# Rolling the columns of an 8192 x 8192 matrix: the heads of the rows spread over the copy

## The chip, the cores and the metric

One core of one Trainium2 chip runs the kernel. The metric is the device time of one execution in microseconds; the time before is the median of three runs.

## The reference

The input is a float32 matrix of 8192 x 8192 (268 MB), rolled by 100 columns to the right:

```python
def setup_inputs():
    return {"x": np.random.randn(8192, 8192).astype(np.float32), "shift": 100}

def reference(x, shift):
    return np.roll(x, shift, axis=1)
```

So `out[r, 100:8192] = x[r, 0:8092]` and `out[r, 0:100] = x[r, 8092:8192]`. Nothing is calculated; 268.44 MB are read and 268.44 MB are written.

## The kernel before

With `s = 100`, the kernel sets `a = 256`: of each output row, the columns from 256 on are the "long piece" (7936 columns, 31.7 KB), and the first 256 columns, 1 KB, are the "head". `g = a - s = 156` is how many columns of the head come from the start of the same input row; the other 100 come from the end of it.

**The copy of long pieces (L36 to L43).** It goes from DRAM to DRAM directly. Rows are taken in `blocks = 128` blocks of 64 rows. A block is four transfers (`j`), each of 16 rows, with SP issuing the even ones and ACT the odd ones (`engines[j % 2]`). So each queue issues two 496 KB transfers to a block. In the last four blocks each transfer is cut in two at column `mid`. There are 528 transfers in all, and each of the two engines issues its own in order.

**The heads (L60 to L80).** POOL issues all their transfers, and they go through SBUF. A stage `k` is 512 rows: 128 partitions of `Q = 4` neighbouring rows, and there are `n_st = 16` stages. The end of row r and the start of row r + 1 lie side by side in memory, so one read can take both.

- L72 reads into tile `t` three pieces of 1 KB for each partition: the last 100 columns of a row together with the first 156 of the next (384 KB).
- L73 reads the last 100 columns of the partition's fourth row into tile `h` (50 KB), and L76 the first 156 columns of its first row (78 KB).
- L74 and L77, two copies on DVE, put the two parts of each piece of `t` into their places in `h`. `h` is then four heads of 1 KB for each partition.
- L80 stores `h` into the first 256 columns of 512 output rows (512 KB).

The stages' reads are all issued first, in one loop (L67 to L78), and the stores after them in a second loop (L79, L80). Each pool has 16 buffers, one for each stage, so that no stage waits for the buffers of another. POOL runs its instructions in the order of the program. In the program all copies of long pieces stand ahead of all heads; since they are on other engines, the heads start at once, beside the copy.

Of the kernel before, what the change touches and what calls it, by code (L numbers as in the profile page):

```python
# [1 line left out]

# [4 lines left out]


@with_exitstack
def kernel(  # L10
    ctx: ExitStack,
    tc: tile.TileContext,
    x: bass.AP,
    shift: int,
    out: bass.AP,
):
    nc = tc.nc
    n_rows, n_cols = x.shape
    s = shift % n_cols
    a = -(-s // 128) * 128  # L20
    if 0 < a <= 384 and a + 128 <= n_cols:
        a += 128
    g = a - s
    P = nc.NUM_PARTITIONS
    engines = [nc.sync, nc.scalar]
    n_chunks = 16
    rows = n_rows // n_chunks

    xm = x.rearrange("(c e j) w -> c j e w", e=16, j=4)
    om = out.rearrange("(c e j) w -> c j e w", e=16, j=4)
    if a < n_cols:  # L36
        blocks = n_rows // 64
        mid = (a + n_cols) // 256 * 128
        for c in range(blocks):
            parts = ((a, mid), (mid, n_cols)) if c >= blocks - 4 and a < mid else ((a, n_cols),)  # L40
            for j in range(4):
                for lo, hi in parts:
                    engines[j % 2].dma_start(out=om[c, j, :, lo:hi], in_=xm[c, j, :, lo - s:hi - s])  # L43
    if a == 0:
        return


    if a > 512:
        for i in range(n_chunks):
            r = slice(i * rows, (i + 1) * rows)  # L50
            nc.gpsimd.dma_start(out=out[r, :s], in_=x[r, n_cols - s:])
            if g > 0:
                nc.gpsimd.dma_start(out=out[r, s:a], in_=x[r, :g])
        return

    Q = 4  # L60
    n_st = n_rows // (P * Q)
    reads = ctx.enter_context(tc.tile_pool(name="reads", bufs=n_st))
    heads = ctx.enter_context(tc.tile_pool(name="heads", bufs=n_st))
    xt = x.rearrange("(k p q) c -> k p q c", q=Q, p=P)
    ot = out.rearrange("(k p q) c -> k p q c", q=Q, p=P)
    tiles = []
    for k in range(n_st):  # L67
        t = reads.tile([P, Q - 1, a], x.dtype)
        h = heads.tile([P, Q, a], x.dtype)
        lead = bass.AP(tensor=x.tensor, offset=(k * P * Q + 1) * n_cols - s,  # L70
                       ap=[[Q * n_cols, P], [n_cols, Q - 1], [1, a]])
        nc.gpsimd.dma_start(out=t[:], in_=lead)  # L72
        nc.gpsimd.dma_start(out=h[:, Q - 1, :s], in_=xt[k, :, Q - 1, n_cols - s:])  # L73
        nc.vector.tensor_copy(h[:, :Q - 1, :s], t[:, :, :s])  # L74
        if g > 0:
            nc.gpsimd.dma_start(out=h[:, 0, s:], in_=xt[k, :, 0, :g])  # L76
            nc.vector.tensor_copy(h[:, 1:, s:], t[:, :, s:])  # L77
        tiles.append(h)  # L78
    for k, h in enumerate(tiles):  # L79
        nc.gpsimd.dma_start(out=ot[k, :, :, :a], in_=h[:])  # L80


# [1 line left out]
_INS = ['x', 'shift']  # L84
_OUTS = [((8192, 8192), 'float32')]

_NUMBERS = {'shift': 100}


# [26 lines left out]
```

## Time and profile before

| | |
|---|---|
| time, median of 3 runs | 816.8 us (815.75 to 818.27) |
| span of the profiled execution | 828.0 us |
| instructions in the profile | 689 |
| DMA packets | 22278, 276.90 MB, mean 334 GB/s |
| first and last read of heads issued (L72) | 1.3 and 240.4 us |
| first and last store of heads issued (L80) | 242.2 and 379.6 us |
| long piece of 496 KB, issue to landing, median | 12.7 us |
| read into `t`, issue to landing, median | 50.6 us |
| store of `h`, issue to landing, median | 108.2 us |
| POOL busy | 41.3 us; an L72 762 ns, L73 559 ns, L76 542 ns, L80 724 ns on average |
| DVE busy | 12.3 us; L74 382 ns, L77 467 ns on average |

The profiled execution is one of its own; its span is 1.4% over the median of the runs. Times within it are counted from the span's start. A DMA queue's row gives packets, megabytes and the time its packets took as a share of what 16 DMA engines have in the span: q1 and q10 carry the long pieces of SP and ACT, and q0 carries what POOL issues. GB/s in the profile counts each byte moved once, so a byte that goes from DRAM to DRAM counts once though it is read and written there. A row of waits names the waiting instruction, what it waited for, the microseconds in total, how many times, and the longest.

### The profile page before, as it was taken

How to read it: one execution, taken by the hardware profiler on the slowest of the kernel's cores; microseconds unless marked ns; L12 is line 12 of the kernel's file. 1: busy time of each engine (PE TensorE's matmuls, PEld its weight loads, DVE VectorE, ACT ScalarE, POOL GpSimd, SP SyncE). 2: the span in 40 equal slices, each digit the busy share in tenths (PEclk: the TensorE clock that was granted, in tenths of full speed). 3: DMA queues.
4: the chain of work that ended last, by engine and by line, in shares of the span. 5: the costliest groups of instructions: out<-in, count | busy, mean ns of one | idle time of the engine just before them, and what ended most of it. 6: DMA issues, size and time to landing. Idle time of an engine off the chain costs nothing. (4 is left out here: it accounts for less than half of the span.)

```text
span 828.0 us, 689 instructions
## 1 busy us (share of the span) xinstructions
DVE 12.3 (1%) x32; POOL 41.3 (5%) x68
## 2 busy tenths in 40 slices
DVE  0000000000010000000000000000000000000000
POOL 2011000000021100000000000000000000000000
DMA  9999999999999999999999999999999999999998
GB/s 308 340 350 334 344 340 337 337 339 344 337 342 348 352 351 345 354 339 346 347 341 344 333 325 325 319 330 333 330 324 322 335 330 328 322 331 328 327 314 300
DMA packets 22278, 276.90 MB, mean 334 GB/s; under 512 B 9473, under 2 KB 9729, under 8 KB 13825
## 3 DMA queue, kind: packets, MB, share of 16 engines
q1 hardware_dynamic: 8448, 130.04, 46.1%
q10 hardware_dynamic: 8448, 130.04, 44.7%
q0 software_dynamic: 5376, 16.78, 8.4%
q14 instruction: 6, 0.04, 0.0%
HBM read 268.44 MB, written 268.44 MB: 648 GB/s over the span
## 5 line engine op out<-in xcount | busy, mean ns | idle before, releaser
L80 POOL DMA_DIRECT2D out_dram<-h x16 | 11.5, 724 | 126.6 <-DMA out_dram<-h 86.8
L76 POOL DMA_DIRECT2D h<-in_x_dram x16 | 8.7, 542 | 141.4 <-DMA t<-in_x_dram 141.4
L72 POOL DMA_DIRECT2D t<-in_x_dram x16 | 12.2, 762 | 30.8 <-DMA h<-in_x_dram 30.0
L73 POOL DMA_DIRECT2D h<-in_x_dram x16 | 8.9, 559 | 39.9 <-DMA h<-in_x_dram 39.9
L74 DVE COPY h<-t 128x300 f32<-128x300 f32 x16 | 6.1, 382 | 260.2 <-DMA t<-in_x_dram 260.2
L77 DVE COPY h<-t 128x468 f32<-128x468 f32 x16 | 7.5, 467 | 0.0
L97 POOL MEMSET const-float32-0.0<- 128x1 f32 x1 | 0.1, 99 | 0.2 <-issue 0.2
L97 POOL MEMSET const-bfloat16-1.0<- 128x1 bf16 x1 | 0.1, 102 | 0.0
L97 POOL MEMSET const-float32-1.0<- 128x1 f32 x1 | 0.1, 99 | 0.0
L97 POOL MEMSET const-uint8-127<- 128x1 uint8 x1 | 0.1, 99 | 0.0
## 6 DMA issues: line engine op xcount, KB each, us to landing
out_dram<-in_x_dram ACTq DMA_DIRECT2D x248, 496.0 KB, 12.7
out_dram<-in_x_dram SPq DMA_DIRECT2D x248, 496.0 KB, 12.7
out_dram<-h POOLq DMA_DIRECT2D x16, 512.0 KB, 108.2
t<-in_x_dram POOLq DMA_DIRECT2D x16, 384.0 KB, 50.6
out_dram<-in_x_dram SPq DMA_DIRECT2D x16, 248.0 KB, 6.0
out_dram<-in_x_dram ACTq DMA_DIRECT2D x16, 248.0 KB, 5.9
h<-in_x_dram POOLq DMA_DIRECT2D x16, 78.0 KB, 43.2
h<-in_x_dram POOLq DMA_DIRECT2D x16, 50.0 KB, 49.9
```

The lines of the kernel that those rows point to most:

```text
L72: nc.gpsimd.dma_start(out=t[:], in_=lead)
L73: nc.gpsimd.dma_start(out=h[:, Q - 1, :s], in_=xt[k, :, Q - 1, n_cols - s:])
L74: nc.vector.tensor_copy(h[:, :Q - 1, :s], t[:, :, :s])
L76: nc.gpsimd.dma_start(out=h[:, 0, s:], in_=xt[k, :, 0, :g])
L77: nc.vector.tensor_copy(h[:, 1:, s:], t[:, :, s:])
L80: nc.gpsimd.dma_start(out=ot[k, :, :, :a], in_=h[:])
L97: nc = _bacc.Bacc("TRN2", target_bir_lowering=False, num_devices=1)
```

## The change

The loop over blocks and the two loops over stages become one. The copies of a block are put into a helper, `copies(c)`, which returns the last transfer of the block. Reads of a stage are put into `fetch(k, ins)`. After the copies of blocks 3, 10, 17 and so on to 115 (`first = 3`, `step = (128 - 6) // 17 = 7`, so 17 times), POOL gets the store of the stage before and the reads of the next stage. The store and the first read each get a dependency on the last transfer of that block (`add_manual_dep`), so POOL waits until that transfer has landed. The first time there is no store, the last time there are no reads. The pools have 3 buffers instead of 16. The shapes of all transfers and the way in which rows and columns are divided stay as they are, as does the cut of the last four blocks. The path for `a == 0` or `a > 512` is written differently, but does not run here.

```diff
-    if a < n_cols:
-        blocks = n_rows // 64
-        mid = (a + n_cols) // 256 * 128
+    blocks = n_rows // 64
+    mid = (a + n_cols) // 256 * 128
+
+    def copies(c):
+
+        last = None
+        parts = ((a, mid), (mid, n_cols)) if c >= blocks - 4 and a < mid else ((a, n_cols),)
+        for j in range(4):
+            for lo, hi in parts:
+                if lo < hi:
+                    last = engines[j % 2].dma_start(out=om[c, j, :, lo:hi], in_=xm[c, j, :, lo - s:hi - s])
+        return last
...
-    reads = ctx.enter_context(tc.tile_pool(name="reads", bufs=n_st))
-    heads = ctx.enter_context(tc.tile_pool(name="heads", bufs=n_st))
...
-    tiles = []
-    for k in range(n_st):
+    reads = ctx.enter_context(tc.tile_pool(name="reads", bufs=3))
+    heads = ctx.enter_context(tc.tile_pool(name="heads", bufs=3))
+    after = mybir.DependencyInfo(mybir.DependencyClass.Sync, mybir.DependencyReason.DATA)
+    first = 3
+    step = (blocks - 2 * first) // (n_st + 1)
+
+    def fetch(k, ins):
         t = reads.tile([P, Q - 1, a], x.dtype)
         h = heads.tile([P, Q, a], x.dtype)
...
-        nc.gpsimd.dma_start(out=t[:], in_=lead)
+        d = nc.gpsimd.dma_start(out=t[:], in_=lead)
+        tc.add_manual_dep(d.ins, ins.ins.name, after, reason="pace")
         nc.gpsimd.dma_start(out=h[:, Q - 1, :s], in_=xt[k, :, Q - 1, n_cols - s:])
         nc.vector.tensor_copy(h[:, :Q - 1, :s], t[:, :, :s])
         if g > 0:
             nc.gpsimd.dma_start(out=h[:, 0, s:], in_=xt[k, :, 0, :g])
             nc.vector.tensor_copy(h[:, 1:, s:], t[:, :, s:])
-        tiles.append(h)
-    for k, h in enumerate(tiles):
-        nc.gpsimd.dma_start(out=ot[k, :, :, :a], in_=h[:])
+        return h
+
+    held = None
+    k = 0
+    for c in range(blocks):
+        ins = copies(c)
+        if c == first + (k + 1) * step - step and k <= n_st:
+            if held is not None:
+                d = nc.gpsimd.dma_start(out=ot[k - 1, :, :, :a], in_=held[:])
+                tc.add_manual_dep(d.ins, ins.ins.name, after, reason="pace")
+            held = fetch(k, ins) if k < n_st else None
+            k += 1
```

More of the change, by code (lines that the diff above doesn't have):

```diff
@@ L35 @@
     om = out.rearrange("(c e j) w -> c j e w", e=16, j=4)
-    if a < n_cols:
-        blocks = n_rows // 64
-        mid = (a + n_cols) // 256 * 128
-        for c in range(blocks):
[L40 to L49, printed above, removed]
+    blocks = n_rows // 64
[8 more added lines that the diff above has]
+        return last
+    if a == 0 or a > 512:
+        for c in range(blocks):
+            copies(c)
+        for i in range(n_chunks if a else 0):
             r = slice(i * rows, (i + 1) * rows)
```

## The prediction

> **What bounds the kernel now.** I read the page first (busy time, slices, queues), then the busy time by stretch with the queues of each stretch, then the waits of POOL and the order of time around the stores. The page:
>
> ```profile
> DVE 12.3 (1%) x32; POOL 41.3 (5%) x68
> DMA  9999999999999999999999999999999999999998
> q1 hardware_dynamic: 8448, 130.04, 46.1%
> q10 hardware_dynamic: 8448, 130.04, 44.7%
> q0 software_dynamic: 5376, 16.78, 8.4%
> HBM read 268.44 MB, written 268.44 MB: 648 GB/s over the span
> ```
>
> No engine computes to speak of. The DMA engines are busy from the first slice to the last; q1 and q10 are the long pieces that SP and ACT issue, q0 the heads that POOL issues, and the three shares make 99.2%. So the kernel is a fixed amount of traffic, 536.88 MB, and its time is that traffic by the rate at which it is served. The busy time in five stretches (length, DVE, POOL, clock, DMA share, GB/s) shows when heads are in flight:
>
> ```profile
> 0.00:20.00 20.00, 0.75 (x2) 5.86 (x13) 1.00 0.92 306
> 20.00:244.00 224.00, 10.00 (x26) 24.72 (x40) 1.00 1.00 341
> 244.00:488.00 244.00, 1.50 (x4) 10.74 (x15) 1.00 1.01 344
> 488.00:800.00 312.00, 0.00 (x0) 0.00 (x0) 1.00 0.99 327
> 800.00:828.00 28.00, 0.00 (x0) 0.00 (x0) 1.00 0.88 301
> ```
>
> From 0 to 244 us heads are read, from 244 to 488 they are stored, and after 488 the copy runs alone. GB/s counts a byte once, whether it comes from HBM and goes to HBM (copy) or has SBUF at one end (heads). The queues of the store stretch (20 to 242 us and 488 to 800 us were read in the same way) split it:
>
> ```profile
> q1 hardware_dynamic: 2361, 37.59, 46.2%
> q10 hardware_dynamic: 2352, 37.30, 43.3%
> q0 software_dynamic: 2577, 9.08, 11.2%
> ```
>
> Counting copy bytes twice and head bytes once, HBM serves (2 x 74.89 + 9.08) / 244 = 651 GB/s there. For the reads (68.48 MB copied, 7.13 MB of q0 in 222 us) it is 649, and for the copy alone (101.97 MB in 312 us) 654. The 341 to 344 against 327 is therefore no better rate: it is the same HBM rate, with some bytes that cost half. Heads cost their bytes and a toll of 0.4 to 0.7%.
>
> **The change part by part.** I keep the sum against the profiled span of 828.0 us. The median of the runs is 816.8, so a profiled microsecond is worth 0.986 of one; what lies around the span isn't shown.
>
> *Traffic.* Nothing is removed or added: 528 copies on SP and ACT, 64 transfers on POOL with the same shapes, 32 copies on DVE. 0 us.
>
> *Two passes become one, paced.* One stage's four transfers are 5376 / 16 = 336 packets, 21 on each of 16 engines. A store alone takes 13.3 us of the queue, because stores follow each other so:
>
> ```profile
> 283.37 0.71 POOL L80 DMA_DIRECT2D out_dram<-h  x1 [8.79 <-DMA out_dram<-h]
> 296.64 0.71 POOL L80 DMA_DIRECT2D out_dram<-h  x1 [12.56 <-DMA out_dram<-h]
> ```
>
> The reads of a stage take 18.8 us (L72 is issued at 61.34 and, nine stages on, at 230.88). After the change a period holds one store and one stage's reads: 32 us of q0. The period is seven blocks. A block takes 6.26 us with the copy alone (199.5 transfers of 496 KB in 312 us, four to a block) and 6.59 with heads (148 in 244 us), on average 828 / 128 = 6.5, so 45 us. Heads are in flight for 32 of every 45 us, in all about 16 x 32 = 512 us against 488 now. The same mix with the same toll, spread over more of the span: 0 us if the toll stays. Its price is bounded from both sides. Without any toll, 222 x (654 - 649) / 654 + 244 x (654 - 651) / 654 = 1.7 + 1.1 = 2.8 us are gained; with twice the toll as many are lost. I take 0, since the mixed stretches are the nearest rows.
>
> *The pace waits.* L72's and L80's successors wait for the last transfer of block 3, 10, 17 and so on to 115. Queued behind the waiting instruction on POOL are only the rest of that stage: two h reads, and the next stage. DVE waits for them (260.2 us now, in which nothing is late). SP and ACT issue only long pieces and wait for none of it, nor do they pass anything. Cost 0, under cover of the copy. The waits that go are POOL's on earlier transfers:
>
> ```profile
> POOL h L76 <- DMA t<-in_x_dram: 141.4, 13, 14.6
> POOL out_dram L80 <- DMA out_dram<-h: 86.8, 7, 15.6
> ```
>
> They were hidden under the copy too, so their end gains nothing. POOL's 64 issues of 0.54 to 0.76 us remain.
>
> *Three pairs of buffers.* Stage k takes the buffers of stage k-3, whose store was issued two periods, 90 us, earlier. With 13.3 us for a store in the queue this wait doesn't appear. Even if a store took today's 108.2 us to land, the reads would be 18 us late, and their store has 45 - 19 = 26 us to spare. 0 us.
>
> *The end.* Block 115 lands some 12 blocks before the end: 828 - 12 x 6.3 - 3 = about 750 us. The last store then needs 13.3 us, lands near 765 and leaves 60 us of copy alone. The tail is as now (0.88 busy in the last 28 us, with the split blocks), and so is the start (0.92 in the first 20 us). 0 us.
>
> The sum is 828.0 + 0, or 816.8 us as a median.
>
> One rule speaks against putting the store late. The Trainium skill, DMA: Bandwidth & Descriptors, section Rules for kernel authors, says to issue a DMA early and wait for it late, so that the fixed cost overlaps. The row has stores landing 108 us after issue, which would make it the third rival's sum; the interval of 13.3 us makes it the sum above.
>
> And one bears on the ceiling. The Trainium skill, HBM Reference, section Specifications, gives a pair's domain about 716 GB/s; the trace's 654 GB/s is below that. By it the traffic could take 750 us at the least, an estimate from that page, so a better mix isn't excluded, but no stretch here shows one near it.
>
> **The rivals.**
>
> *Thin heads lose their toll (faster).* Heads now stay in flight with up to eight transfers behind each other, and the 16 parts of one transfer drift apart: the last store's parts land from 432.8 to 491.8 us. Short bursts with 13 us of pause let the engines come together. For it: the stretch from 260 to 340 us moved 24.42 MB of copy and 3.72 MB of heads, (48.84 + 3.72) / 80 = 657 GB/s, above the copy alone. Against it: the copy alone, with no heads to drift, has only 654. Price: from 2.8 us (no toll) to the whole middle of 780 us at 657 instead of its mean of 651.6, 780 x 5.4 / 657 = 6.4 us. In the middle 4.6 x 0.986 = 4.5, giving 812.3 us.
>
> *The mix is worse beside its own rows (slower).* Place: each period's burst, in which a store and reads now share q0, in the rows that the copy is passing: stage k is rows 512k to 512k + 511, and the copy is at 448k + 192 when it starts. Today heads run far ahead of the copy and reads and stores overlap for a few us only. For it: reads do have slow stretches; 80 to 100 us moved 6.07 MB of copy and 0.63 of heads, 638.5 GB/s. Against it: 260 to 272 us already holds both kinds, at 358 GB/s moved from 260 to 280. Price: 512 us at 638.5 instead of 651 is 512 x 12.5 / 651 = 9.8 us, as far as 826.5; half way, 4.9 x 0.986 = 4.8, is 821.6 us. It decides from a rate of 648 in the bursts (2.45 us).
>
> *The last store ends the kernel (slower).* With 108.2 us to landing, as the median of the stores is now, it would be there at 750 + 0.7 + 108 = 859 us, 31 late: 847 us as a median. It decides from 78 us on. Against it: the 108 is eight stores queued one behind another, and 8 x 13.3 = 106; the last one will have none ahead of it.
>
> *The pacing doesn't take.* If the waits were put so that heads ran as early as now, only the overlap of store and reads would change, and the copy hides it: 816.8 us.
>
> **How the numbers follow.** A measurement of this kernel can tell 0.3%, 2.45 us, from no change (its three runs span 815.75 to 818.27). Chances: no change 0.42, thin heads 0.30, worse mix 0.22, late last store 0.03, no pacing 0.03. That gives faster 0.30, same 0.45, slower 0.25. The likeliest is 816.8 us with its own range of 814.1 to 819.6 (the toll gone or doubled). For 8 in 10 the range goes down to 811 (the best stretch everywhere would be 810.5) and up to 823 (a good half of the worse mix).
>
> **What would show it.** Right: POOL's issues at some 45 us from each other out to 750 us; the GB/s of the slices even, near 338, with the high first half gone; DMA busy 9 throughout; stores landing within 40 us; q0's packets and bytes unchanged; the last 60 us at 327. The thin-heads case shows as over 654 GB/s at HBM in the paced stretch, the worse mix as under 648, the late store as q0 packets in the last slice. I am wrong if heads' traffic is not priced by its bytes: if the rate at HBM in a paced stretch leaves 648 to 654.

## The result, and the profile after

The changed kernel takes 819.84 us (median of 19 runs, 818.34 to 823.49) where the kernel before takes 817.34 us beside it (19 runs, 815.75 to 820.31). The ratio is 1.0034, with a 95% interval of 1.0023 to 1.0044: slower by about 2.8 us (2.5 by the medians). The time lies within the predicted range, but the forecast was no change, and the step that priced the heads at nothing more than before was wrong.

The page of the changed kernel (parts 1 to 3: busy engines, DMA busy share and GB/s by slices, queues with packets, MB and share of 16 engines):

```profile
span 816.6 us, 730 instructions
DVE 12.0 (1%) x32; POOL 41.7 (5%) x68
DMA  9999999999999999999999999999999999999998
GB/s 307 330 352 323 359 339 342 335 350 345 344 336 344 342 329 353 333 345 341 350 334 353 342 334 346 343 351 327 346 342 345 341 347 342 340 339 338 341 315 298
q1 hardware_dynamic: 8448, 130.04, 46.1%
q10 hardware_dynamic: 8448, 130.04, 44.1%
q0 software_dynamic: 5376, 16.78, 8.5%
HBM read 268.44 MB, written 268.44 MB: 657 GB/s over the span
```

The same row of the kernel before was:

```profile
GB/s 308 340 350 334 344 340 337 337 339 344 337 342 348 352 351 345 354 339 346 347 341 344 333 325 325 319 330 333 330 324 322 335 330 328 322 331 328 327 314 300
```

The traffic is what it was. The high first half of the GB/s row is gone and the row is even up to the 38th slice: the heads are spread, as the change says. The order of time on POOL (start, length, line, idle time before it and what ended it) shows the pacing:

```profile
121.22 0.72 POOL L84 DMA_DIRECT2D out_dram<-h  x1 [22.81 <-DMA out_dram<-in_x_dram]
121.87 0.82 POOL L69 DMA_DIRECT2D t<-in_x_dram  x1
141.28 0.58 POOL L71 DMA_DIRECT2D h<-in_x_dram  x1 [18.59 <-DMA out_dram<-h]
141.85 0.56 POOL L74 DMA_DIRECT2D h<-in_x_dram  x1
165.26 0.72 POOL L84 DMA_DIRECT2D out_dram<-h  x1 [22.85 <-DMA out_dram<-in_x_dram]
...
745.15 0.74 POOL L84 DMA_DIRECT2D out_dram<-h  x1 [43.63 <-DMA out_dram<-in_x_dram]
```

A store and a read into `t` go out every 44 us, and the last store at 745 us. The two reads into `h` stand elsewhere than in the text of the kernel: they wait about 19 us for the store just issued, since they belong to a later stage that takes over its buffer. With three pairs of buffers, the scheduler put them ahead of the next paced wait. The waits of POOL (us in total, times, longest) confirm it:

```profile
POOL out_dram L84 <- DMA out_dram<-in_x_dram: 401.3, 15, 43.6
POOL h L71 <- DMA out_dram<-h: 247.8, 13, 20.2
```

The span of this execution, 816.6 us, is shorter than the 828.0 us on which the prediction was worked out, though the kernel is slower. Spans of single executions can't be compared to a third of a per cent; medians over many runs can, and the traces are used for where a rate is low. A rate from one execution has the same weakness: two stretches of copy alone in one trace (a4 below) have 665 and 662 GB/s.

### The profile page after: what moved, and what is told of

It is laid out like the page before. It is cut to its first block, busy times and chain, and to the rows that moved or that the text cites. A ratio compares the mean times of both kernels' runs of the same rounds, so it can differ in the third digit from the quotient of the medians.

```text
span 816.6 us, 730 instructions
## 1 busy us (share of the span) xinstructions
DVE 12.0 (1%) x32; POOL 41.7 (5%) x68
## 3 DMA queue, kind: packets, MB, share of 16 engines
q0 software_dynamic: 5376, 16.78, 8.5%
## 4 chain that ended last, share of the span: by engine, by line
DMA 91%; ACTq 0%; issue 0%; POOLq 0%
DMA out_dram<-in_x_dram 91%; ACTq L41 0%; POOLq L118 0%; POOLq L84 0%
## 5 line engine op out<-in xcount | busy, mean ns | idle before, releaser
L84 POOL DMA_DIRECT2D out_dram<-h x16 | 11.6, 727 | 427.1 <-DMA out_dram<-in_x_dram 401.3
L71 POOL DMA_DIRECT2D h<-in_x_dram x16 | 9.3, 584 | 248.7 <-DMA out_dram<-h 247.8
## 6 DMA issues: line engine op xcount, KB each, us to landing
out_dram<-h POOLq DMA_DIRECT2D x16, 512.0 KB, 20.4
```

The costliest lines, as they stand in the source:

```text
L84: d = nc.gpsimd.dma_start(out=ot[k - 1, :, :, :a], in_=held[:])
```

## The experiments

HBM rates below are worked out as in the prediction: copy bytes (q1 and q10) twice, head bytes (q0) once, by the length of the stretch. Ratios are to the kernel before, run on the same chip beside each group.

**The kernel before once more.**

> The kernel before against itself, so that a difference of 0.3% can be trusted and a second profile of it can stand beside that of the changed kernel (the first had a span of 828.0 us, 1.3% over the median of the runs). Every theory: ratio 1.000 within 0.001, span near 816 us. The stretch with heads and the stretch of copy alone then show HBM rates (copy bytes twice, head bytes once) near 660 GB/s, as the changed kernel's 20 to 750 us do (249.35 MB moved, (2 x 233.32 + 15.99) / 730 = 661).

817.65 us, ratio 0.9995 (0.9983 to 1.0007), span 815.6 us. Its queues from 20 to 250 us (reads), 250 to 490 us (mostly stores) and 490 to 750 us (copy alone but for the last 23 packets of heads):

```profile
q1 hardware_dynamic: 2261, 35.94, 41.3%
q10 hardware_dynamic: 2261, 35.94, 39.4%
q0 software_dynamic: 2850, 7.75, 19.0%
...
q1 hardware_dynamic: 2379, 37.75, 46.7%
q10 hardware_dynamic: 2375, 37.68, 43.2%
q0 software_dynamic: 2373, 8.50, 10.3%
...
q10 hardware_dynamic: 2715, 43.08, 49.8%
q1 hardware_dynamic: 2714, 43.11, 49.5%
q0 software_dynamic: 23, 0.08, 0.1%
```

That is (2 x 71.88 + 7.75) / 230 = 659, then 664, then 663 GB/s. In this execution the toll (the HBM time that heads cost over that of their bytes) lies with the reads alone; stores cost only their bytes. The 828.0 us execution had shown 649, 651 and 654 and so had put a toll on both. The changed kernel's queues from 250 to 490 us are:

```profile
q1 hardware_dynamic: 2409, 38.29, 45.8%
q10 hardware_dynamic: 2410, 38.26, 43.8%
q0 software_dynamic: 1754, 5.52, 9.5%
```

They give (2 x 76.55 + 5.52) / 240 = 661 GB/s; from 20 to 250 us it is (2 x 73.59 + 4.72) / 230 = 660 and from 490 to 700 us (2 x 67.02 + 4.83) / 210 = 661: below the 663 to 664 that the kernel before has without reads, all the way, though by no more than two stretches of one trace can differ. What the loss lies with is therefore read from the times of the runs below.

**Heads far from the rows of the copy.**

```diff
     def fetch(k, ins):
+        k = (k + 8) % n_st
...
-                d = nc.gpsimd.dma_start(out=ot[k - 1, :, :, :a], in_=held[:])
+                d = nc.gpsimd.dma_start(out=ot[(k + 7) % n_st, :, :, :a], in_=held[:])
```

> The changed kernel with the stages turned by eight (stage k moves the heads of rows 512 ((k + 8) mod 16) and on), so that heads are paced as before but never in rows that the copy is passing. Theory 'own rows': the 2.8 us go away, ratio 1.000. Theory 'thin backlog' (POOL's queue is short or empty in a part of every period, and an engine that is ahead of the others has no head packet to serve meanwhile) and theory 'late heads' (heads in flight up to 765 us disturb the copy's end): the ratio stays at 1.003.

819.26 us, ratio 1.0019 (1.0005 to 1.0033). The loss doesn't go away, so neighbouring rows aren't the whole of it. The interval overlaps that of the changed kernel, and leaves room for a part of it.

**No pace, but three pairs of buffers.**

```diff
-        d = nc.gpsimd.dma_start(out=t[:], in_=lead)
-        tc.add_manual_dep(d.ins, ins.ins.name, after, reason="pace")
+        nc.gpsimd.dma_start(out=t[:], in_=lead)
...
-                tc.add_manual_dep(d.ins, ins.ins.name, after, reason="pace")
```

> The changed kernel without the two dependencies on the copy: three pairs of buffers, each stage's store ahead of the next stage's reads, but POOL goes as fast as its transfers land. Heads end near 500 us. Theory 'thin backlog': between the two, as three pairs of buffers keep the queue fuller than pacing does, but emptier than sixteen: 1.000 to 1.002. Theory 'late heads' and theory 'own rows' (the heads run ahead of the copy): 1.000. If the buffers or the mixing of stores and reads cost the 2.8 us, and not the pacing: 1.003.

818.6 us, ratio 1.0014 (0.9999 to 1.0028), between the two, and not clearly apart from either. The last read into `t` is used at 459 us, where the kernel before is at 290 and the changed one at 735.

**The copy alone.**

```diff
-    for k in range(n_st):
+    for k in range(0):
```

> The long pieces alone; the first 256 columns of every output row are left out. 520.2 MB of HBM traffic instead of 536.9. If heads cost their bytes, the time falls by 16.78 / 536.88 = 3.1%, to 791.8 us (ratio 0.969). If heads cost a toll on top, it falls further: with 2.8 us of toll to 789 us (0.965). If heads fill time that engines would lose without them (theory 'thin backlog'), it falls less: above 794 us (0.972).

789.77 us, ratio 0.9658 (0.9637 to 0.9680). The heads of the kernel before cost 817.51 - 789.77 = 27.7 us, and their bytes 16.78 MB / 664 GB/s = 25.3. The toll is 2.5 us, near the prediction's 2.8; the interval of this run leaves it uncertain by about 1.8 us. In the changed kernel, 2.5 us slower, it has about doubled.

**Half and double the queue of long pieces.** The theory at this point was "dry engines": the 16 DMA engines drift apart, and one that is ahead runs out of queued copy.

```diff
-            parts = ((a, mid), (mid, n_cols)) if c >= blocks - 4 and a < mid else ((a, n_cols),)
+            parts = ((a, mid), (mid, n_cols))
```

> The kernel before with every block's long pieces cut in two at column mid (248 KB instead of 496 KB), as only the last four blocks were. SP and ACT still wait on the transfer four before, so the copy that is queued ahead of each DMA engine is half as long. Theory 'dry engines' (an engine ahead of the others runs out of queued long pieces, and heads in POOL's queue give it something to do meanwhile; pacing takes them away for a part of each period): idle time grows, most in the stretch of copy alone; ratio 1.005 to 1.03. Theory 'mix' (the paced mix is served at a lower HBM rate, engines are never dry): ratio within 0.3% of 1.000.

> The changed kernel with the same cut. To be read against b1_small_before: theory 'dry engines' expects the gap between the two to grow from 2.8 us to 6 us or more, with DMA shares that add to less; theory 'mix' expects it to stay near 2.8 us.

821.89 us, 1.0048 (1.0029 to 1.0067), and 821.42 us, 1.0047 (1.0034 to 1.0060): no gap is measured, to about 2 us, where one of 6 us or more was expected.

```diff
+            if c < blocks - 4:
+                for j in range(2):
+                    engines[j].dma_start(out=ob[c, :, j::2, a:], in_=xb[c, :, j::2, a - s:n_cols - s])
+                continue
```

> The kernel before with two of a block's transfers joined (992 KB, the same rows on the same engine; the last four blocks as before). Four such are in flight, so twice as much copy is queued ahead. Theory 'dry engines': the three shares, 99.0% in the kernel before, rise to 99.5% or more and the time falls by 2 to 5 us (ratio 0.994 to 0.998). Theory 'mix': 1.000.

> The changed kernel with the same joining. Read against b3_big_before: theory 'dry engines' expects the gap of 2.8 us to close to under 1 us; theory 'mix' expects 2.8 us.

826.1 us, 1.0104 (1.0086 to 1.0123), and 825.45 us, 1.0085 (1.0073 to 1.0097). Both kernels are slower, and there is again no gap to the paced one's disadvantage. The busy slices and GB/s of the joined kernel before show where it loses:

```profile
DMA  9999999999999999999999999999999999999958
GB/s 311 342 339 337 346 334 343 351 331 348 346 332 341 344 340 334 339 344 357 342 348 353 337 353 347 341 346 346 340 341 339 328 328 331 330 335 328 325 198 284
```

Most of the loss is at the end: the 39th slice is half busy. The first and the last of the 16 parts of one long piece arrive 18 us apart in this trace (median), against 6 in the kernel before; that some engines are done long before the others at the end fits this, but the trace doesn't tell the engines apart. With the longer queue nothing is gained before the end either. "Dry engines", as stated, failed at both sizes.

**Reads alone and stores alone.** Each half of the heads, free (as in the kernel before) and paced. The edits of c1 and c4 are shown; c2 and c3 leave out the same part of the other kernel:

```diff
-        nc.gpsimd.dma_start(out=ot[k, :, :, :a], in_=h[:])
+        pass
```

> The kernel before with its head reads and without the sixteen stores (the first 256 columns of every row are left out). Copy alone took 789.8 us; 8.39 MB more at the 664 GB/s of its middle are 12.6 us, so 802.4 us (ratio 0.9815) if reads cost only their bytes. The profile of the kernel before has 658 GB/s while it reads, 1% under the copy alone, over 230 us: 2.3 us of toll, 804.7 us (0.984). All theories expect this one; it is the base for c2_reads_paced.

> The changed kernel with its paced reads and without the stores. Theory 'reads cost more when paced' (folded over a period, the changed kernel's HBM rate is lowest, 618 to 658 GB/s, in the 16 us after the store, when the read into t is in flight): c1_reads_free + 2.8 us, about 807.5 (0.988). Theory 'the mix of both kinds' (either kind alone is harmless): equal to c1_reads_free within 1 us. Theory 'stores cost more when paced': equal too.

```diff
+    zero = heads.tile([P, Q, a], x.dtype)
+    nc.vector.memset(zero[:], 0.0)
...
     def fetch(k, ins):
-        t = reads.tile([P, Q - 1, a], x.dtype)
...
-        return h
+        return zero
```

> The kernel before with the sixteen stores (of one tile of zeros) and without any head read. By the profile of the kernel before, whose stretch with stores runs at the 664 GB/s of the copy alone, stores cost only their bytes: 802.4 us (0.9815). All theories.

> The changed kernel with its paced stores (of one tile of zeros) and without any head read. Theory 'stores cost more when paced': c3_stores_free + 2.8 us, 805.2 (0.985). Theories 'reads cost more when paced' and 'the mix of both kinds': equal to c3_stores_free within 1 us.

| | free | paced | paced less free |
|---|---|---|---|
| reads only | 805.39 us, 0.9851 (0.9834 to 0.9869) | 808.42 us, 0.9894 (0.9877 to 0.9911) | 3.0 us |
| stores only | 801.50 us, 0.9803 (0.9787 to 0.9819) | 802.45 us, 0.9814 (0.9798 to 0.9831) | 1.0 us, intervals overlap |

The loss lies with the reads. The queues from 490 to 700 us, first with free reads, which are all done by then, and then with paced ones:

```profile
q1 hardware_dynamic: 2212, 35.11, 50.8%
q10 hardware_dynamic: 2209, 35.05, 48.4%
```

```profile
q1 hardware_dynamic: 2138, 33.91, 47.2%
q10 hardware_dynamic: 2144, 34.00, 45.9%
q0 software_dynamic: 732, 2.13, 5.2%
```

2 x 70.16 / 210 = 668 GB/s against (2 x 67.91 + 2.13) / 210 = 657. The free reads, while they run (20 to 250 us), have 659; the paced ones 659, 656 and 657 in all three stretches. At a third of the bytes in the same time, the rate is as low. Two things weaken the 668 against 657. The profiled execution of c1 was the fastest of its five (803.22 us) and that of c2 the slowest (810.97), so this difference is larger than the 3.0 us of the medians; inside c1's own trace the step is from 659 to 664 (250 to 490 us). And the shares make 98.3% in c2 against 99.2% in c1, so in these two runs idle engines go along with the lower rate.

**Early reads, paced stores.**

```diff
-    reads = ctx.enter_context(tc.tile_pool(name="reads", bufs=3))
-    heads = ctx.enter_context(tc.tile_pool(name="heads", bufs=3))
+    reads = ctx.enter_context(tc.tile_pool(name="reads", bufs=n_st))
+    heads = ctx.enter_context(tc.tile_pool(name="heads", bufs=n_st))
...
-        d = nc.gpsimd.dma_start(out=t[:], in_=lead)
-        tc.add_manual_dep(d.ins, ins.ins.name, after, reason="pace")
+        nc.gpsimd.dma_start(out=t[:], in_=lead)
...
+    early = [fetch(k) for k in range(n_st)]
...
-            held = fetch(k, ins) if k < n_st else None
+            held = early[k] if k < n_st else None
```

> The changed kernel with its sixteen stores paced as they are, but all reads at the start as in the kernel before (16 pairs of buffers). Theory 'paced reads' (of the 2.8 us, some 3.0 us lie with the reads by c1 and c2, and 1.0 us or nothing with the stores by c3 and c4): 817 to 818.5 us, ratio 1.000 to 1.001. If pacing the stores, or the mere presence of heads late in the copy, were the cause: 819.8 us, 1.0034.

817.79 us, ratio 1.0005 (0.9993 to 1.0018), apart from the changed kernel's 1.0023 to 1.0044. With the reads back at the start the loss is gone, although the stores stay paced to the same end. In the whole kernel, too, it is the reads. This kernel has 16 pairs of buffers again, so that the pace of the reads and the three pairs are undone together; a wait for a store's buffer isn't needed for the loss, since c2 waits for no store and loses 3.0 us against c1.

**Finer reads.**

```diff
+        if n < 3:
+            lead = bass.AP(tensor=x.tensor, offset=(k * P * Q + 1 + n) * n_cols - s,
+                           ap=[[Q * n_cols, P], [1, a]])
+            paced(t[:, n, :], lead, ins)
+        elif n == 3:
+            paced(h[:, Q - 1, :s], xt[k, :, Q - 1, n_cols - s:], ins)
```

> The changed kernel with each stage's reads spread over its period: the read into t in three parts of 128 KB after the first, second and third block, the two reads into h after the fourth and fifth, the store as it was. Theory 'dry after a burst' (a burst of reads drives the 16 engines apart, and when POOL's queue is empty the engines that are ahead have nothing queued: c2's busy share folded over the period is 0.93 to 0.97 in the 12 us after the burst): smaller bursts cost less, 817 to 818.5 us, ratio 1.000 to 1.001. Theory 'toll of company' (a read beside the copy costs HBM time whenever heads and copy run together for long): still 819.8 us, 1.003.

819.81 us, ratio 1.0031 (1.0020 to 1.0042): nothing is gained. Its queues from 250 to 490 us:

```profile
q10 hardware_dynamic: 2401, 38.10, 46.4%
q1 hardware_dynamic: 2405, 38.19, 43.7%
q0 software_dynamic: 1958, 5.68, 9.4%
```

The shares make 99.5%, against 99.1% in the changed kernel, so the engines aren't dry; but the rate is (2 x 76.29 + 5.68) / 240 = 659 GB/s and the time is the same. Idle engines don't explain the loss of the whole kernel. Nor does the wait of the reads into `h` for a store, since here every read is paced by the copy itself.

**Twice the reads.**

```diff
+        u = reads.tile([P, Q - 1, a], x.dtype)
+        d = nc.gpsimd.dma_start(out=u[:], in_=lead)
+        tc.add_manual_dep(d.ins, ins.ins.name, after, reason="pace")
```

> c2_reads_paced with each stage's read into t issued twice, the second time into a tile that nobody uses (6.29 MB more, no stores). Read against d4: if the price of paced reads grows with what is read in a burst, the gap to d4 is 3.0 x 14.68 / 8.39 = 5.3 us; if a fixed price for a pause or a wait, it stays at 3.0 us.

> c1_reads_free with the same doubling. 805.4 us plus 6.29 MB at 658 GB/s: 815 us (ratio 0.997). All theories; it is the base for d3.

Paced 817.98 us, 1.0012 (0.9997 to 1.0026); free 817.02 us, 1.0000 (0.9988 to 1.0012). With more bytes the gap does not grow to 5.3 us; its estimate falls to 1.0 us, and the intervals overlap. What did change is how long the free reads last: the last read into `t` is used at 450 us instead of 246, and the paced ones' at 719 and 715.

**The shape of the reads.** Other data than the heads are fetched here.

```diff
-        lead = bass.AP(tensor=x.tensor, offset=(k * P * Q + 1) * n_cols - s,
-                       ap=[[Q * n_cols, P], [n_cols, Q - 1], [1, a]])
+        lead = bass.AP(tensor=x.tensor, offset=(k * P * Q + 1) * n_cols,
+                       ap=[[Q * n_cols, P], [n_cols, Q - 1], [1, a]])
```

> c2_reads_paced with every head read starting on a multiple of 1 KB of the input's row (columns 0 to 255 for the read into t, 100 columns from 7936 on for the fourth row), so that other data than the heads are fetched; pieces, counts, rows and pacing as in c2, no stores. If the crooked start of the pieces (400 bytes ahead of a row) is what makes paced reads dear: from 808.4 us down toward the free reads' 805.4 or the bytes' 802.4. If not: 808.4 us (ratio 0.989).

809.65 us, ratio 0.9893 (0.9872 to 0.9914): the crooked start is not the cause. With one piece of 3 KB in place of three of 1 KB:

```diff
-                       ap=[[Q * n_cols, P], [n_cols, Q - 1], [1, a]])
+                       ap=[[Q * n_cols, P], [a, Q - 1], [1, a]])
```

> e1_aligned_reads with the read into t taking one piece of 3 KB from one row for each partition instead of three of 1 KB from three rows; bytes, transfers and pacing as in c2, no stores. If the number of pieces or of rows makes paced reads dear: toward 802.4 us (ratio 0.982). If reads beside the copy cost by the time that they are in flight, whatever their shape: 808.4 us (0.989).

805.42 us, ratio 0.9846 (0.9826 to 0.9865), apart from c2's 0.9877 to 0.9911. It is apart from e1's interval as well, from which it differs by this edit alone. The same bytes, paced in the same way, but in longer pieces, cost 3 to 4 us less: as little as the free reads. Whether it is the length of a piece, or that a partition now reads from one row instead of three, isn't separated. Its queues from 490 to 700 us:

```profile
q10 hardware_dynamic: 2155, 34.32, 46.9%
q1 hardware_dynamic: 2152, 34.10, 47.2%
q0 software_dynamic: 636, 2.36, 5.2%
```

(2 x 68.42 + 2.36) / 210 = 663 GB/s, where c2's short pieces had 657 (in its slowest execution).

**What the runs come to.** At this size of long piece, the times fit a toll of short head reads that goes by how long they are in flight, and not by their bytes. In flight means here from issue to landing, read from each trace, with time in which several reads overlap counted once. The toll in the table is an estimate: the run's ratio less that of the copy alone (0.9658), times 817.4 us, less the reads' bytes at 664 GB/s.

| run | bytes read | reads in flight | toll | toll for 100 us |
|---|---|---|---|---|
| c1, free | 8.39 MB | 250 us | 3.1 us | 1.2 us |
| d4, free, doubled | 14.68 MB | 467 us | 5.9 us | 1.3 us |
| c2, paced | 8.39 MB | 515 us | 6.7 us | 1.3 us |
| d3, paced, doubled | 14.68 MB | 603 us | 6.8 us | 1.1 us |

Paced reads of 8.39 and of 14.68 MB have the same toll, and the free ones double theirs with their time. That fits the small gap between d3 and d4: doubled free reads are in flight nearly as long as paced ones. A fixed price for each burst or pause would fit c2 and d3, but not d4 against c1, nor d2, whose smaller and more numerous bursts cost the same as the changed kernel's. The 3 KB pieces of e2, by the same working, have 2.7 us in 462. With the stores in the kernel it is alike: reads are in flight for 297 us in the kernel before (a1), 464 in a3 and 635 in the changed kernel. The differences of medians are 2.5 us for 337 us more (the change), 1.1 for 167 (a3), 3.0 for 265 (c2 less c1) and 1.0 for 136 (d3 less d4): 0.7 to 1.1 us for 100 us. Each difference is uncertain by 1 to 2 us, and the interval of the copy alone would move all tolls of the table together by up to 1.8 us, so this is a rule of thumb and no law.

It is not shown at the other sizes. With cut pieces the reads are in flight 208 us longer in the paced kernel (305 against 97 us), worth about 2 us by the rule; the measured gap is -0.5 us, uncertain by 2, which decides nothing. With joined pieces they are in flight 309 us longer (735 against 426), worth about 3 us, and the paced kernel is no slower: there the rule fails.

Two things stay open: by what mechanism a few short reads slow the copy beside them, and why it doesn't show in b3 and b4, where both kernels lose time by the size of the piece itself. That nearness of rows has a part of it (a2) isn't excluded either.

## Why the prediction was right or wrong

*What bounds the kernel: right.* The time is HBM traffic by its rate. The copy alone took 789.77 us; the reads add their bytes and a small toll, and the stores no more than their bytes (801.50 us in c3).

*"Two passes become one, paced": this step failed.* It took "the same mix with the same toll" at 0 us. The toll was taken to stay as long as bytes and mix stay; the runs show that it lies with the reads (3.0 us between c1 and c2, and gone with early reads in d1) and goes with the time for which they are in flight, which pacing stretches from 297 to 635 us. By what mechanism they do so stays open. The bound beside it, twice the toll, 2.8 us lost, is what was measured, but no reason was given for a doubled toll: that the time lies at this bound is luck. The nearest rows misled in three ways. The execution at hand was 1.4% over the median of the runs and spread the toll over reads (649) and stores (651 against 654 GB/s); a second one shows it with the reads alone (659 against 664 and 663). The step called 512 us of heads against 488 "the same", though only the reads count: until 735 us against 290. And 512 was too low: it took 13.3 us for a store from the spacing of stores queued one behind another, while a single one lands 20.4 us after issue, and the reads into `h` go out behind it, so that heads of some kind were in flight for 666 us.

*The pace waits: right.* They are 401.3 us of POOL's time before stores, and they cost nothing by themselves: with the stores paced and the reads early (d1), where POOL waits 409.7 us, nothing measurable is lost.

*Three pairs of buffers: wrong in the wait, not shown to cost.* The wait that "doesn't appear" is there 13 times, 247.8 us in all, because the reads into `h` were moved ahead of the paced wait and queue for a buffer that a store has just begun to empty. In d2 each read is paced by the copy instead, and the time is the same.

*The end: right.* The last store goes out at 745 us, and stores land in 20.4 us, so the late-store rival didn't happen. The rule of the Trainium skill (DMA: Bandwidth & Descriptors, section Rules for kernel authors) that a DMA is to be issued early, so that its fixed cost overlaps, was weighed there against a late store. No run here shows such a fixed cost. Issuing the reads early does pay, 817.79 us in d1 against 819.84, but because of the toll above.

*The rivals.* "Thin heads lose their toll" had the sign wrong: thinner reads keep their toll for longer. "The mix is worse beside its own rows" had the sign right, the price too high (4.8 us at its middle) and a place that a2 supports at most in part. Of its two kinds, no cost of the stores beyond their bytes is shown.

*The signs named in advance misled.* A rate over 654 GB/s in the paced stretch was to mean thin heads, and so a faster kernel. The changed kernel has 660 to 661 there and is slower: the limits of 648 and 654 came from the 828.0 us execution, and a1 has 659 to 664.

## What to carry to other kernels

A transfer that rides beside a saturated copy isn't priced by its bytes alone: find out with reads alone and stores alone which of them carries the toll, and whether it grows with bytes or with the time in flight, before spreading it out. If it is time, do the dear kind early and densely and pace only the cheap kind. Before a mixed stretch is used as a price, see that the profiled execution's span agrees with the median of the runs; one that is 1.4% over can put a toll in the wrong place.

## What the runs showed of the hardware

- Head reads in pieces of 1 KB, beside the copy, cost an estimated 1.1 to 1.3 us for each 100 us in flight, whether they move 34 GB/s (c1, 20 to 250 us) or 10 to 13 (c2). In single traces HBM has 656 to 659 GB/s with them and 662 to 668 for copy alone (a1, a4, c1). Pieces of 3 KB had 663 (e2), and stores of 1 KB pieces 664 to 665 even when paced (c4).
- More copy queued ahead made the kernel slower, not faster: with 992 KB transfers the parts of one piece arrived 18 us apart (median; 6 with 496 KB) and the ratio was 1.0104 (1.0086 to 1.0123), most of the loss in the last two slices.
- Busier DMA queues didn't mean a shorter time: finely paced reads had shares of 99.5% from 250 to 490 us, against 99.1% in the changed kernel, and took 819.81 against 819.84 us.
